# Column sums of a 32768 x 2048 array: adds folded in halves, loads on the GpSimd queue, column blocks on TensorE column groups

## The chip, the cores and the metric

The kernel runs on one core of a Trainium2 chip. The metric is the device time of one execution in microseconds (us).

## The reference

The input `grad_output` has the shape 32 x 1024 x 2048 in fp32 (268.4 MB). The output is the sum over the first two axes, one value for each of 2048 columns:

```
np.sum(grad_output, axis=(0, 1)).astype(np.float32)
```

In what follows the input is a matrix of 32768 rows and D = 2048 columns. A "row" in the text is 128 of these, one in each SBUF partition: 8 KB a partition, 1.05 MB in all. There are 256 such rows.

## The kernel before, in words

**Loads.** 31 bulk loads of 8 rows each (64 KB a partition, contiguous in memory; L69) go out from the SP queue, then a tail of 4, 2 and 1 rows (L87), and a last row in four quarters of 512 columns (L97). A pool gives three buffers of 8 rows (L34); the tail and the last row share one of them. A load into a buffer waits until all that read its earlier content is done.

**Adds.** VectorE keeps one accumulator `acc` of 128 x 2048. For each row of a bulk tile it adds the row to `acc` (L79 for the first, L81 for the others): 8 adds of 2048 columns a tile, and 3 in the last bulk tile.

**TensorE.** What VectorE leaves is summed over the partitions, and added up, by matmuls with a matrix of ones (`mm`, L49 and L50): the last 5 rows of the last bulk tile (`PE_ROWS_LAST`), the 7 tail rows, `acc` and the last row. `sum_row` (L56 to L63) cuts a row into SPLIT = 4 quarters and each quarter into GROUPS = 4 pieces of C = 128 columns. Piece g of each quarter goes to column group g of TensorE, which is PSUM partitions 32 g to 32 g + 31. All four groups so get 384 columns for `head` and 128 for `last` of each row. The ones are 128 x 32, and the 32 output partitions of a group hold the same sums. An fp32 matmul stands in the trace as two, each with its weight load.

**Order.** Each queue runs its instructions in the order of the program, and the framework puts in the waits between engines. On TensorE the order is that of the source: 5 rows of the last bulk tile, 4 tail rows, `acc` (L93), the 2 and the 1 tail rows, then the quarters of the last row as they land.

**End.** ScalarE copies `head` (L105) and VectorE `last` (L106) to `res`, and two stores, from the ScalarE queue (L108) and from SP (L111), write one partition of each group to the output.

Of the kernel before, what the change touches and what calls it, by code (L numbers as in the profile page):

```python
# [1 line left out]

# [4 lines left out]

P = 128
ROWS = 8  # L10
GROUPS = 4
SPLIT = 4
TAIL = (4, 2, 1)
PE_ROWS_LAST = 5


@with_exitstack
def kernel(
    ctx: ExitStack,
    tc: tile.TileContext,  # L20
    grad_output: bass.AP,
    out: bass.AP,
):
    nc = tc.nc
    fp32 = mybir.dt.float32
    D = out.shape[-1]
    flat = grad_output.rearrange("b s d -> (b s) d")
    R = flat.shape[0]
    W = D // SPLIT
    C = W // GROUPS  # L30
    n_bulk = (R // P - sum(TAIL) - 1) // ROWS
    assert (n_bulk * ROWS + sum(TAIL) + 1) * P == R

    io_pool = ctx.enter_context(tc.tile_pool(name="io", bufs=3))  # L34
    const_pool = ctx.enter_context(tc.tile_pool(name="const", bufs=1))
    psum_pool = ctx.enter_context(tc.tile_pool(name="psum", bufs=1, space=bass.MemoryType.PSUM))

    ones = const_pool.tile([P, 32], fp32)
    nc.vector.memset(ones[:], 1.0)  # L39
    acc = const_pool.tile([P, D], fp32)  # L40


    head = psum_pool.tile([P, (SPLIT - 1) * C], fp32)
    last = psum_pool.tile([P, C], fp32)
    res = const_pool.tile([P, SPLIT * C], fp32)

    started = set()

    def mm(dst, g, src, stop):  # L49
        nc.tensor.matmul(  # L50
            dst, lhsT=ones[:], rhs=src, start=(g not in started), stop=stop,
            skip_group_check=True,
        )
        started.add(g)

    def sum_row(src):  # L56
        v = src.rearrange("p (k g i) -> p k g i", k=SPLIT, g=GROUPS)
        for g in range(GROUPS):
            q = slice(32 * g, 32 * g + 32)
            mm(head[q, :].rearrange("p (k i) -> p k i", i=C), ("h", g), v[:, : SPLIT - 1, g, :], False)  # L60
        for g in range(GROUPS):
            q = slice(32 * g, 32 * g + 32)
            mm(last[q, :], ("l", g), v[:, SPLIT - 1, g, :], False)  # L63

    row = 0
    for t in range(n_bulk):
        T = io_pool.tile([P, ROWS * D], fp32, tag="T", name=f"t{t}")
        src = flat[row : row + P * ROWS].rearrange("(p m) d -> p (m d)", p=P)
        nc.sync.dma_start(out=T[:], in_=src)  # L69
        row += P * ROWS  # L70
        on_pe = PE_ROWS_LAST if t == n_bulk - 1 else 0
        for j in range(ROWS):
            part = T[:, j * D : (j + 1) * D]
            if j >= ROWS - on_pe:
                sum_row(part)
            elif t == 0 and j == 0:
                continue
            elif t == 0 and j == 1:
                nc.vector.tensor_add(out=acc[:], in0=T[:, :D], in1=part)  # L79
            else:  # L80
                nc.vector.tensor_add(out=acc[:], in0=acc[:], in1=part)  # L81

    T = io_pool.tile([P, ROWS * D], fp32, tag="T", name="tail")
    at = 0
    for i, m in enumerate(TAIL):
        src = flat[row : row + P * m].rearrange("(p m) d -> p (m d)", p=P)
        nc.sync.dma_start(out=T[:, at * D : (at + m) * D], in_=src)  # L87
        row += P * m
        for j in range(m):
            sum_row(T[:, (at + j) * D : (at + j + 1) * D])  # L90
        at += m
        if i == 0:
            sum_row(acc[:])  # L93

    for k in range(SPLIT):
        dst = T[:, at * D + k * W : at * D + (k + 1) * W]
        nc.sync.dma_start(out=dst, in_=flat[row : row + P, k * W : (k + 1) * W])  # L97
        for g in range(GROUPS):
            q = slice(32 * g, 32 * g + 32)
            into = head[q, k * C : (k + 1) * C] if k < SPLIT - 1 else last[q, :]  # L100
            mm(into, ("h" if k < SPLIT - 1 else "l", g), dst[:, g * C : (g + 1) * C], k >= SPLIT - 2)

    o = out.rearrange("(k g i) -> g k i", k=SPLIT, g=GROUPS)
    n = (SPLIT - 1) * C
    nc.scalar.copy(out=res[:, :n], in_=head[:])  # L105
    nc.vector.tensor_copy(out=res[:, n:], in_=last[:])  # L106
    rows = res[:].rearrange("(g r) c -> g r c", r=32)[:, 0, :]
    nc.scalar.dma_start(  # L108
        out=o[:, : SPLIT - 1, :], in_=rows[:, :n].rearrange("g (k i) -> g k i", i=C)
    )  # L110
    nc.sync.dma_start(out=o[:, SPLIT - 1, :], in_=rows[:, n:])  # L111


# [1 line left out]
_INS = ['grad_output']  # L115
_OUTS = [((2048,), 'float32')]


# [23 lines left out]
```

## Time and profile before

| what | value |
|---|---|
| median of 10 runs | 630.09 us (629.85 to 630.75) |
| the profiled execution's own time | 630.49 us |
| its span, from the first to the last instruction | 628.6 us |
| VectorE busy | 555.0 us (88%), 244 instructions |
| TensorE busy (matmuls) | 16.6 us (3%), 240 instructions |
| data queue (q1), share of the 16 DMA engines' time | 98.9% |
| read from memory | 268.44 MB, 427 GB/s over the span |
| first load's landing | 22.70 us |
| last load's landing | 624.87 us |
| median time from a bulk load's issue to its landing | 39.4 us |

The profile is of one execution. Its span leaves out what lies around the first and the last instruction, so the execution's own time is 1.89 us longer. PE is TensorE's matmuls, PEld its weight loads, DVE is VectorE, ACT ScalarE, POOL GpSimd, SP SyncE; L81 is line 81 of the kernel. A group of instructions reads: line, engine, operation, out<-in, shapes, count, busy time and mean of one in ns, idle time of the engine just before, and what ended most of it.

### The profile page before, as it was taken

What the parts mean: (1) busy time and instruction counts of PE and PEld (TensorE: products, weight loads), DVE (VectorE), ACT (ScalarE), POOL (GpSimd) and SP (SyncE); (2) the same over time, 40 slices, a digit from 0 to 9 for tenths busy, and PEclk for the clock granted to TensorE, in tenths of its full rate; (3) what the DMA queues carried; (4) which work ended last, traced back from release to release, by engine and by line L of the source; (5) the groups of instructions that cost most, each with busy time, mean ns of one, the idle gap of its engine ahead of it and who ended that gap; (6) DMA issues with size and microseconds to landing.
All of it is one profiled execution on the core that took longest, in us unless ns stands there. A gap on an engine that the chain in (4) does not pass through costs nothing.

```text
span 628.6 us, 874 instructions
## 1 busy us (share of the span) xinstructions
PE 16.6 (3%) x240; PEld 8.5 (1%) x240; DVE 555.0 (88%) x244; ACT 1.8 (0%) x2; POOL 0.2 (0%) x4
## 2 busy tenths in 40 slices
PE   0000000000000000000000000000000000000046
PEld 0000000000000000000000000000000000000023
DVE  0579999999899999999999999999999999999980
ACT  0000000000000000000000000000000000000000
POOL 0000000000000000000000000000000000000000
PEclk9999999999999999999999999999999999999998
DMA  9999999999999999999999999999999999999996
GB/s 400 409 459 409 459 417 450 417 450 418 446 421 446 421 446 413 455 413 455 413 455 413 455 413 455 409 459 401 467 400 467 400 467 400 467 400 467 400 432 242
DMA packets 5500, 268.50 MB, mean 427 GB/s; under 512 B 616, under 2 KB 632, under 8 KB 1144
## 3 DMA queue, kind: packets, MB, share of 16 engines
q1 hardware_dynamic: 5480, 268.44, 98.9%
q8 instruction: 2, 0.03, 0.0%
q14 instruction: 2, 0.02, 0.0%
q10 hardware_dynamic: 16, 0.01, 0.0%
HBM read 268.44 MB, written 0.01 MB: 427 GB/s over the span
## 4 chain that ended last, share of the span: by engine, by line
DMA 69%; DVE 29%; issue 0%; SPq 0%; PE 0%; DVEq 0%
DMA t<-in_grad_output_dram 63%; DVE acc L81 29%; DMA tail<-in_grad_output_dram 6%; SPq L97 0%; SPq L87 0%; PE last L50 0%; SPq L69 0%; DVE res L106 0%; DVEq L81 0%
## 5 line engine op out<-in xcount | busy, mean ns | idle before, releaser
L81 DVE TENSOR_TENSOR acc<-acc,t 128x2048 f32<-128x2048 f32 x241 | 552.3, 2292 | 34.9 <-DMA t<-in_grad_output_dram 27.7
L50 PE MATMUL head<-t,ones 128*32 128x384 f32 x40 | 5.9, 661 | 605.3 <-DMA t<-in_grad_output_dram 605.3
L79 DVE TENSOR_TENSOR acc<-t 128x2048 f32<-128x2048 f32 x1 | 2.3, 2291 | 21.8 <-DMA t<-in_grad_output_dram 21.8
L106 DVE COPY res<-last 128x128 f32<-128x128 f32 x1 | 0.3, 293 | 13.2 <-PE last L50 13.2
L50 PEld LDWEIGHTS head<-t,ones 128*32 128x32 f32 x40 | 1.6, 143 | 605.3 <-DVE acc L81 605.3
L50 PE MATMUL head<-tail,ones 128*32 128x384 f32 (+1 forms) x80 | 8.3, 497 | 3.2 <-DMA tail<-in_grad_output_dram 3.1
L50 PE MATMUL last<-tail,ones 128*32 128x128 f32 x64 | 3.8, 311 | 0.2 <-DMA tail<-in_grad_output_dram 0.2
L50 PEld LDWEIGHTS head<-tail,ones 128*32 128x32 f32 x80 | 2.6, 123 | 3.8 <-DMA tail<-in_grad_output_dram 3.8
L50 PE MATMUL last<-t,ones 128*32 128x128 f32 x40 | 2.6, 332 | 0.0
L50 PEld LDWEIGHTS last<-tail,ones 128*32 128x32 f32 x64 | 2.3, 127 | 4.1 <-issue 3.6
L105 ACT COPY res<-head 128x384 f32<-128x384 f32 x1 | 0.5, 478 | 622.8 <-PE head L50 622.8
L50 PEld LDWEIGHTS last<-t,ones 128*32 128x32 f32 x40 | 1.7, 137 | 3.0 <-issue 3.0
L105 ACT ACT_TABLE_LOAD x1 | 1.3, 1283 | 0.7 <-PEq L126 0.7
L50 PE MATMUL head<-acc,ones 128*32 128x384 f32 x8 | 0.8, 486 | 0.0
L39 DVE MEMSET ones<- 128x32 f32 x1 | 0.1, 85 | 0.8 <-PEq L126 0.8
L50 PE MATMUL last<-acc,ones 128*32 128x128 f32 x8 | 0.4, 272 | 0.0
L50 PEld LDWEIGHTS last<-acc,ones 128*32 128x32 f32 x8 | 0.3, 110 | 0.4 <-issue 0.4
L50 PEld LDWEIGHTS head<-acc,ones 128*32 128x32 f32 x8 | 0.2, 110 | 0.0
L126 POOL MEMSET const-bfloat16-1.0<- 128x1 bf16 x1 | 0.1, 102 | 0.0
L126 POOL MEMSET const-uint8-127<- 128x1 uint8 x1 | 0.1, 102 | 0.0
L126 POOL MEMSET const-float32-1.0<- 128x1 f32 x1 | 0.1, 99 | 0.0
L126 POOL MEMSET const-float32-0.0<- 128x1 f32 x1 | 0.1, 98 | 0.2 <-issue 0.2
## 6 DMA issues: line engine op xcount, KB each, us to landing
tail<-in_grad_output_dram SPq DMA_DIRECT2D x1, 4096.0 KB
tail<-in_grad_output_dram SPq DMA_DIRECT2D x1, 2048.0 KB, 34.2
tail<-in_grad_output_dram SPq DMA_DIRECT2D x1, 1024.0 KB, 36.3
tail<-in_grad_output_dram SPq DMA_DIRECT2D x4, 256.0 KB, 36.7
t<-in_grad_output_dram SPq DMA_DIRECT2D x31, 39.4
out_dram<-res ACTq DMA_DIRECT2D x1, 6.0 KB
out_dram<-res SPq DMA_DIRECT2D x1, 2.0 KB
```

What stands on the lines that cost most here:

```text
L39: nc.vector.memset(ones[:], 1.0)
L50: nc.tensor.matmul(dst, lhsT=ones[:], rhs=src, start=(g not in started), stop=stop, skip_group_check=True,)
L79: nc.vector.tensor_add(out=acc[:], in0=T[:, :D], in1=part)
L81: nc.vector.tensor_add(out=acc[:], in0=acc[:], in1=part)
L105: nc.scalar.copy(out=res[:, :n], in_=head[:])
L106: nc.vector.tensor_copy(out=res[:, n:], in_=last[:])
L126: nc = _bacc.Bacc("TRN2", target_bir_lowering=False, num_devices=1)
```

## The change

The work is divided anew.

- *Loads.* 26 tiles of 8 rows, then tiles of 7, 7, 6, 6, 5, 5, 4 and 2 rows (`FOLDED`), a tile of 3 rows (`DIRECT`) and the last 3 rows. The first tile's load stays on SP; all others are issued from the GpSimd queue. The buffers are still three; each of these tiles takes one, and the last 3 rows take one together.
- *Adds.* VectorE folds each tile in place: one wide instruction adds the second half of its rows to the first half, and so on, until one row is left (for 8 rows: 4, 2 and 1 rows wide), and adds this one to `acc`. For odd counts the middle row stays for the next step. The first tile's last fold writes `acc`. In all there are 132 adds; before there were 242.
- *TensorE.* The ones are 128 x 1, so a result has one partition. Of the columns, 0 to 511 go to column group 1, 512 to 1023 to group 2, 1024 to 1535 to group 3 (`LEFT`), 1536 to 1791 to group 0 and 1792 to 2047 to group 1 (`RIGHT`), each block in a PSUM bank of its own. TensorE sums the 3 `DIRECT` rows, then `acc`, then the last 3 rows. The last 3 come as four loads: columns 0 to 1535 of two rows and of one row, then columns 1536 to 2047 of two rows and of one row; their matmuls are in the order left, then right.
- *End.* ScalarE copies blocks 0, 2 and 4 and VectorE blocks 1 and 3 into partition 0 of `acc`, and one store from SP writes the 8 KB. A copy of one element at the start makes ScalarE load its table there.

```
--- before.py
+++ after.py
@@ -7,11 +7,14 @@
 from concourse._compat import with_exitstack
 
 P = 128
-ROWS = 8
-GROUPS = 4
-SPLIT = 4
-TAIL = (4, 2, 1)
-PE_ROWS_LAST = 5
+
+
+
+FOLDED = (8,) * 26 + (7, 7, 6, 6, 5, 5, 4, 2)
+DIRECT = (3,)
+LAST = 3
+LEFT = ((0, 512, 1), (512, 512, 2), (1024, 512, 3))
+RIGHT = ((1536, 256, 0), (1792, 256, 1))
 
 
 @with_exitstack
@@ -26,89 +29,84 @@
     D = out.shape[-1]
     flat = grad_output.rearrange("b s d -> (b s) d")
     R = flat.shape[0]
-    W = D // SPLIT
-    C = W // GROUPS
-    n_bulk = (R // P - sum(TAIL) - 1) // ROWS
-    assert (n_bulk * ROWS + sum(TAIL) + 1) * P == R
+    assert (sum(FOLDED) + sum(DIRECT) + LAST) * P == R
 
     io_pool = ctx.enter_context(tc.tile_pool(name="io", bufs=3))
     const_pool = ctx.enter_context(tc.tile_pool(name="const", bufs=1))
     psum_pool = ctx.enter_context(tc.tile_pool(name="psum", bufs=1, space=bass.MemoryType.PSUM))
 
-    ones = const_pool.tile([P, 32], fp32)
+    ones = const_pool.tile([P, 1], fp32)
     nc.vector.memset(ones[:], 1.0)
+    warm = const_pool.tile([1, 1], fp32)
+    nc.scalar.copy(out=warm[:], in_=ones[0:1, :])
     acc = const_pool.tile([P, D], fp32)
 
 
-    head = psum_pool.tile([P, (SPLIT - 1) * C], fp32)
-    last = psum_pool.tile([P, C], fp32)
-    res = const_pool.tile([P, SPLIT * C], fp32)
 
+    sums = {}
+    for b, (lo, n, g) in enumerate(LEFT + RIGHT):
+        bank = psum_pool.tile([P, 512], fp32, tag=f"ps{b}", name=f"ps{b}")
+        sums[lo] = bank[32 * g : 32 * g + 1, :n]
     started = set()
 
-    def mm(dst, g, src, stop):
-        nc.tensor.matmul(
-            dst, lhsT=ones[:], rhs=src, start=(g not in started), stop=stop,
-            skip_group_check=True,
-        )
-        started.add(g)
-
-    def sum_row(src):
-        v = src.rearrange("p (k g i) -> p k g i", k=SPLIT, g=GROUPS)
-        for g in range(GROUPS):
-            q = slice(32 * g, 32 * g + 32)
-            mm(head[q, :].rearrange("p (k i) -> p k i", i=C), ("h", g), v[:, : SPLIT - 1, g, :], False)
-        for g in range(GROUPS):
-            q = slice(32 * g, 32 * g + 32)
-            mm(last[q, :], ("l", g), v[:, SPLIT - 1, g, :], False)
+    def add(src, pieces, base=0, stop=False):
+        for lo, n, g in pieces:
+            nc.tensor.matmul(
+                sums[lo], lhsT=ones[:], rhs=src[:, lo - base : lo - base + n],
+                start=(lo not in started), stop=stop,
+            )
+            started.add(lo)
 
     row = 0
-    for t in range(n_bulk):
-        T = io_pool.tile([P, ROWS * D], fp32, tag="T", name=f"t{t}")
-        src = flat[row : row + P * ROWS].rearrange("(p m) d -> p (m d)", p=P)
-        nc.sync.dma_start(out=T[:], in_=src)
-        row += P * ROWS
-        on_pe = PE_ROWS_LAST if t == n_bulk - 1 else 0
-        for j in range(ROWS):
-            part = T[:, j * D : (j + 1) * D]
-            if j >= ROWS - on_pe:
-                sum_row(part)
-            elif t == 0 and j == 0:
-                continue
-            elif t == 0 and j == 1:
-                nc.vector.tensor_add(out=acc[:], in0=T[:, :D], in1=part)
-            else:
-                nc.vector.tensor_add(out=acc[:], in0=acc[:], in1=part)
 
-    T = io_pool.tile([P, ROWS * D], fp32, tag="T", name="tail")
-    at = 0
-    for i, m in enumerate(TAIL):
-        src = flat[row : row + P * m].rearrange("(p m) d -> p (m d)", p=P)
-        nc.sync.dma_start(out=T[:, at * D : (at + m) * D], in_=src)
-        row += P * m
+    def load(m, lo=0, hi=D, at=None, advance=True, queue=None):
+        nonlocal row
+        n = hi - lo
+        if at is None:
+            at = io_pool.tile([P, 8 * D], fp32, tag="T", name=f"t{row}_{lo}")[:, : m * n]
+        src = flat[row : row + P * m].rearrange("(p m) d -> p m d", p=P)[:, :, lo:hi]
+        (queue or nc.gpsimd).dma_start(out=at.rearrange("p (m d) -> p m d", m=m), in_=src)
+        if advance:
+            row += P * m
+        return at
+
+    for i, m in enumerate(FOLDED):
+        T = load(m, queue=nc.sync if i == 0 else None)
+        while m > 1:
+            h = m // 2
+            into = acc[:] if i == 0 and m == 2 else T[:, : h * D]
+            nc.vector.tensor_add(out=into, in0=T[:, : h * D], in1=T[:, (m - h) * D : m * D])
+            m -= h
+        if i:
+            nc.vector.tensor_add(out=acc[:], in0=acc[:], in1=T[:, :D])
+
+    for m in DIRECT:
+        T = load(m)
         for j in range(m):
-            sum_row(T[:, (at + j) * D : (at + j + 1) * D])
-        at += m
-        if i == 0:
-            sum_row(acc[:])
+            add(T[:, j * D : (j + 1) * D], LEFT + RIGHT)
+    add(acc[:], LEFT + RIGHT)
 
-    for k in range(SPLIT):
-        dst = T[:, at * D + k * W : at * D + (k + 1) * W]
-        nc.sync.dma_start(out=dst, in_=flat[row : row + P, k * W : (k + 1) * W])
-        for g in range(GROUPS):
-            q = slice(32 * g, 32 * g + 32)
-            into = head[q, k * C : (k + 1) * C] if k < SPLIT - 1 else last[q, :]
-            mm(into, ("h" if k < SPLIT - 1 else "l", g), dst[:, g * C : (g + 1) * C], k >= SPLIT - 2)
-
-    o = out.rearrange("(k g i) -> g k i", k=SPLIT, g=GROUPS)
-    n = (SPLIT - 1) * C
-    nc.scalar.copy(out=res[:, :n], in_=head[:])
-    nc.vector.tensor_copy(out=res[:, n:], in_=last[:])
-    rows = res[:].rearrange("(g r) c -> g r c", r=32)[:, 0, :]
-    nc.scalar.dma_start(
-        out=o[:, : SPLIT - 1, :], in_=rows[:, :n].rearrange("g (k i) -> g k i", i=C)
-    )
-    nc.sync.dma_start(out=o[:, SPLIT - 1, :], in_=rows[:, n:])
+    T = io_pool.tile([P, 8 * D], fp32, tag="T", name="last")
+    cut, at, left, right = RIGHT[0][0], 0, [], []
+    first = row
+    for lo, hi, into in ((0, cut, left), (cut, D, right)):
+        row = first
+        for m in (LAST - 1, 1):
+            n = hi - lo
+            S = load(m, lo, hi, T[:, at : at + m * n])
+            into += [S[:, j * n : (j + 1) * n] for j in range(m)]
+            at += m * n
+    for j, S in enumerate(left):
+        add(S, LEFT, stop=j == LAST - 1)
+    for j, S in enumerate(right):
+        add(S, RIGHT, base=cut, stop=j == LAST - 1)
+    res = acc[0:1, :]
+    for k, (lo, n, g) in enumerate(LEFT + RIGHT):
+        if k in (0, 2, 4):
+            nc.scalar.copy(out=res[:, lo : lo + n], in_=sums[lo])
+        else:
+            nc.vector.tensor_copy(out=res[:, lo : lo + n], in_=sums[lo])
+    nc.sync.dma_start(out=out[None, :], in_=res)
 
 
 # ---- launch: one core; inputs and outputs as the reference has them ----
```

## The prediction

> **What bounds the kernel now.** I read, in this order: the page's parts 2 to 4, the loads' windows, the waits of the queue and of VectorE, then the timeline of the last 25 us. The page first.
>
> ```profile
> DMA  9999999999999999999999999999999999999996
> DMA packets 5500, 268.50 MB, mean 427 GB/s; under 512 B 616, under 2 KB 632, under 8 KB 1144
> q1 hardware_dynamic: 5480, 268.44, 98.9%
> q8 instruction: 2, 0.03, 0.0%
> q14 instruction: 2, 0.02, 0.0%
> DMA 69%; DVE 29%; issue 0%; SPq 0%; PE 0%; DVEq 0%
> L81 DVE TENSOR_TENSOR acc<-acc,t 128x2048 f32<-128x2048 f32 x241 | 552.3, 2292 | 34.9 <-DMA t<-in_grad_output_dram 27.7
> ```
>
> The 16 DMA engines are busy in every slice but the last. The chain names VectorE for 29%, but only because each new load waits for a buffer; VectorE itself waits for data. The windows (columns: stretch and length; PE, PEld, DVE, ACT, POOL busy; clock; DMA share; GB/s) give the rate of three loads each:
>
> ```profile
> 217.20:275.26 58.06, 0.00 (x0) 0.00 (x0) 55.00 (x24) 0.00 (x0) 0.00 (x0) 1.00 1.00 433
> 391.35:450.38 59.03, 0.00 (x0) 0.00 (x0) 55.00 (x24) 0.00 (x0) 0.00 (x0) 1.00 1.02 443
> ```
>
> 58.05 / 3 = 19.35 us for 8 rows of 1.05 MB, 2.419 us a row. The longer window is one engine's: its landing marks in the trace fall behind the other 15 by 0.98 us at 143 us and again at 434 us, where an 8 KB packet of q14 (VectorE's instructions) stands between its data packets. A load has landed when its last engine has.
>
> ```profile
> SPq L69 <- DVE acc L81: 520.0, 28, 19.0
> DVE acc L81 <- DMA t<-in_grad_output_dram: 27.7, 30, 3.2
> ```
>
> The queue waits up to 19.0 us for VectorE, yet load to landing has a median of 39.4 us: when a buffer comes free, two loads are still under way. So folding faster can't start data sooner. The kernel is bound by its bytes, and only its end is free to move:
>
> ```profile
> 607.02 1.53 PE L50 MATMUL head<-t,ones 128*32 128x384 f32 x8
> 608.73 1.16 PE L50 MATMUL head<-t,ones 128*32 128x384 f32 x8
> 610.78 0.83 PE L50 MATMUL head<-t,ones 128*32 128x384 f32 x8
> 624.91 0.42 PE L50 MATMUL last<-tail,ones 128*32 128x128 f32 x8 [0.20 <-DMA tail<-in_grad_output_dram]
> 625.40 0.29 DVE L106 COPY res<-last 128x128 f32<-128x128 f32 x1 [13.15 <-PE last L50]
> 625.73 0.65 SPq L111 DMA_DIRECT2D out_dram<-res  x1
> ```
>
> One row on TensorE (four column groups at once, 512 columns each) took 608.73 - 607.02 = 1.71 us early, and 0.86 us later (the row ahead of the third line began at 609.92). TensorE kept up: the last data landed at 624.87 and its work was over 0.47 us later. From the last copy's end (625.70) to the span's end (628.6) there are 2.90 us.
>
> **What the Trainium skill says.** "DMA: Bandwidth & Descriptors", section "Issuing engines are not separate DMA queues": loads from any queue run on the same 16 engines. So the move to GpSimd buys no bandwidth by itself. No run here shows a load from that queue; the same page's "Specifications" give it about 1 us to the first byte against 0.6 us. In the trace SP's first load was issued at 0.73 and its first packet started at 1.74 us, 1.0 us.
> "SBUF — State Buffer", section "Who interferes with whom": a two-input add in SBUF doesn't lock GpSimd out of writing descriptors (the page calls this inferred). No run here shows it.
> "TensorE: Matmul & The Clock Gate", Part 1: TensorE runs at half rate until a free-running window of 3.4 us has been busy. The trace agrees: 1.71 us a row until about 609.4, 4.05 us after the first matmul at 605.35, then 0.86.
>
> **The change part by part.**
> *Folding.* 132 adds in place of 242. An add of 2048 columns starts every 2.325 us, of which 2048/0.96 GHz ("VectorE: DVE Perf Modes", Specifications) is 2.133 and 0.192 the fixed part. An 8-row tile is then 8 x 2.133 + 4 x 0.192 = 17.83 us against 18.60. In the bulk this hides under the 19.35 us of the next load: worth nothing.
> *Queue.* 38 loads go from SP to GpSimd; SP keeps the first, so both start together and nothing else of weight stands in either queue. Issue cost is hidden by the two loads under way, as long as it is below 2 x 19.35 - 17.8 = 20.9 us. I leave the packet time at 2.420 us for 64 KB. The new access pattern names the rows one by one; I take it that a partition's rows still go as one packet.
> *Instruction fetches.* 132 adds and their waits are some 165 instructions, so I expect one q14 fetch, not two: 0.98 us saved on the late engine.
> *Shrinking loads.* A tile of m rows costs m x 2.133 + (adds) x 0.192: 15.70 (7), 13.57 (6), 11.43 (5), 9.11 (4), 4.65 (2). Loads stay as in the trace, 2.419 us a row; I start from the late engine's first landing, 22.70, plus one fetch. The second 7-row tile lands at 541.3, and from there VectorE is never idle: it ends at 557.0, 570.6, 584.2, 595.6, 607.1 and, with the 4-row tile, 616.2; acc is ready at 620.8. The three direct rows land at 616.3. **A new wait**: the last load needs the buffer of the 4-row tile, free at 616.2. Reaction of the software queue: unknown; at least SP's 1.0 us, I take 2.0, at most 5. Gap before the last load: 616.2 + 2.0 - 616.3 = 1.9 us. Its 3 rows need 7.26 us and 0.43 more for 48 short packets an engine (a 2 KB packet took 84 ns, an 8 KB one 313, where 37.6 ns a KB would give 75 and 301: 9 ns each). Last byte at 625.8, against 624.87.
> *TensorE.* The column groups are no longer even. A full row gives group 1 two blocks, 512 + 256 columns; groups 2 and 3 get 512, group 0 256. At 0.86/512 = 1.684 ns a column, group 1 sets the pace: (3 direct rows + acc) x 768 + 3 left x 512 + 3 right x 256 = 5376 columns, 9.05 us. It can't start before 616.3 (L93's earlier rows, which in the kernel before gave TensorE work from 605.35 on, are gone), and starts at half rate. That lasts 3.4 us at best (the page), 4.05 in this trace, 6.8 at worst (start just after a window's edge); I take the middle, 5.1, and lose 5.1 x (1 - 0.86/1.71) = 2.5 us. End of TensorE: 616.3 + 0.1 + 9.05 + 2.5 = **627.95**. It is later than the last byte plus a right row (625.8 + 0.43), so the gap of 1.9 us is hidden behind TensorE; if TensorE had less to do, the gap would be next.
> *End.* 0.06 to notice, a copy of 256 columns 0.29 + 128/0.96 GHz = 0.43, then 2.90 as before; the result leaves as one row of 8 KB (a packet of 313 ns, or 16 of 512 B at 25): 0.15. The warm-up copy hides ScalarE's table load at the start, as now. The span ends at 627.95 + 0.06 + 0.43 + 2.90 + 0.15 = 631.5.
> *Sum.* 631.5 - 628.6 = 2.9 us. Profiled execution: 630.49 + 2.9 = 633.4. The median of the runs is 0.40 below that execution: **633.0 us**.
>
> **The rivals.**
> *Shorter packets (17%).* If rows leave as packets of 8 KB, each takes 313 ns instead of 2420/8 = 302.5: 3.5% of 619 us is 21 us, 654 us; at 4 KB the fixed 9 ns counts twice. For it: the access pattern is split by row, and software writes the descriptors. Against: a full row range is contiguous on both sides. If only part of this happens, from 642 us up.
> *GpSimd held up by the wide adds (9%).* If an add does keep GpSimd from its descriptors, the direct load, wanted at 607.1, waits for the 4-row tile's first add (2 x 2.133 + 0.16 = 4.4 us) or its whole 9.1 us. Nothing is left under way to hide it, and TensorE starts that much later: 637.4 to 642. For it: nothing in this trace; against it, the page above.
> *Not slower (17%).* The software queue might hand each engine its next packet without a pause. The page gives the fabric 435.2 GB/s, so 64 KB would take 2.409 us (an estimate from "DMA: Bandwidth & Descriptors", Specifications) rather than 2.420. Up to the direct rows that is 31.6 x 0.075 = 2.4 us: 630.6, no change; with no fetch on the late engine and the shortest cold stretch, 628.8. It decides at about 2.413 us a packet, where 1.6 us are won. Against it: SP's 98.9% leaves little to win.
>
> **How the numbers follow.** Differences of 0.2% (1.26 us) can be told from no change: below 628.8, 628.8 to 631.4, above. My forecast has 57%: 633.0, own range 631.2 to 635 (cold stretch 3.4 to 6.8 us: -0.8 to +0.8; reaction up to 5 us: the last byte then comes at 628.8 and TensorE ends 629.3, +1.3). All of it but 2% is slower. The two slow rivals add 26%; the third splits into 12% same and 5% faster. Slower 0.55 + 0.26 = 0.81, same 0.14, faster 0.05. For 8 in 10 the range takes in the forecast, the held-up GpSimd and most of the no-change case, and leaves out the shorter packets and the faster tail: 629.5 to 642.
>
> **What would show it.** Right: packets of 64 KB at 2.42 us on the new queue; VectorE without idle time from about 541 us; direct rows landing near 616 and TensorE working without a break from then to 2 us after the last byte; a gap of DMA near 616. Wrong: a mean of bytes over time below 420 GB/s in the bulk (short packets); late starts of loads behind wide adds; TensorE waiting for data at the end.

## The result, and the profile after

The changed kernel takes 643.84 us (median of 8 runs, 643.46 to 644.32) against 630.13 us for the kernel before (29 runs): a ratio of 1.0217, 95% interval 1.0208 to 1.0226. It is 2.2% slower, 13.7 us, where 633.0 us was predicted. The span grew from 628.6 to 642.0 us, 13.4 us.

From the page of the changed kernel: the span, DMA's busy tenths in 40 slices and its rate, the packets, the queues (packets, MB, share of the 16 engines' span), and the chain's shares.

```profile
span 642.0 us, 404 instructions
DMA  9997799999999999999999999999999999999995
DMA packets 5684, 268.46 MB, mean 418 GB/s; under 512 B 625, under 2 KB 625, under 8 KB 1201
q0 software_dynamic: 5536, 260.05, 94.1%
q1 hardware_dynamic: 146, 8.40, 3.1%
q14 instruction: 2, 0.02, 0.0%
DMA 60%; DVE 34%; issue 5%; PE 0%; POOL 0%; POOLq 0%
```

The kernel before showed 9s up to the last slice. Here the fourth and fifth slices, 48 to 80 us, are at 7: the DMA engines stood idle early, once. The number of packets hardly changed, and the trace's 64 KB packets on q0 last 2.420 us, as on SP's queue. The loss isn't in the rate of the transfers. The mean of 418 GB/s lies below the 420 that the prediction named as the sign of short packets, but idle time brings it down, not short packets. The windows of the changed kernel show where it is (columns as in the prediction's windows):

```profile
40.00:60.00 20.00, 0.00 (x0) 0.00 (x0) 20.00 (x3) 0.00 (x0) 0.00 (x0) 1.00 0.97 419
61.50:69.40 7.90, 0.00 (x0) 0.00 (x0) 7.90 (x3) 0.00 (x0) 0.53 (x1) 1.00 0.00 0
80.00:100.00 20.00, 0.00 (x0) 0.00 (x0) 19.43 (x6) 0.00 (x0) 1.06 (x2) 1.00 1.03 446
```

For 7.9 us nothing moves, while VectorE is busy throughout. In the trace's landing marks, loads 0 and 1 land at 39.71 and 42.12, load 2 at 61.47 and load 3 at 90.33 us: 28.86 instead of 19.35 us after the one ahead. The timeline of the changed kernel's start (start, duration, engine, line, operation, count, idle time before and its releaser) says why:

```profile
0.74 0.40 SPq L68 DMA_DIRECT2D t<-in_grad_output_dram  x1
1.25 1.20 POOL L68 DMA_DIRECT2D t<-in_grad_output_dram  x2 [0.80 <-POOLq L124]
39.73 25.96 DVE L78 TENSOR_TENSOR t<-t 128x8192 f32<-128x8192 f32 x4 [38.86 <-DMA t<-in_grad_output_dram]
65.61 2.28 DVE L78 TENSOR_TENSOR acc<-t 128x2048 f32<-128x2048 f32 x1
67.82 10.88 DVE L78 TENSOR_TENSOR t<-t 128x2048 f32<-128x2048 f32 x2
68.19 0.53 POOL L68 DMA_DIRECT2D t<-in_grad_output_dram  x1 [65.75 <-DVE acc L78]
```

Tile 0 has three folds, two within `t` and one into `acc`. But *four* stand ahead of the one into `acc`: two of them are tile 1's. VectorE's program after the build isn't in the order of the source. Its beginning (program lines, no profile; t_0_74 is tile 0, t_0_79 tile 1, t_0_85 tile 2):

```
L78 t_0_74<-t_0_74 128x8192
L78 t_0_79<-t_0_79 128x8192
L78 t_0_74<-t_0_74 128x4096
L78 t_0_79<-t_0_79 128x4096
L78 acc<-t_0_74 128x2048
L78 t_0_79<-t_0_79 128x2048
L78 t_0_85<-t_0_85 128x8192
L81 acc<-acc,t_0_79 128x2048
```

From there on each tile is finished before the next, up to the last two folded tiles. Load 3 needs tile 0's buffer. It comes free at 65.61 + 2.28 = 67.89, 6.42 us after load 2 has landed and left nothing under way. GpSimd issues load 3 at 68.19, its first packet starts at 69.42, and the load lands 20.91 us after it, where loads that follow one another land 19.35 us apart: 6.42 + 1.53 + 1.56 = 9.51 us. (The first load of the kernel before, which also started with nothing under way, took 20.96 us from its first packet to its landing.)

The timeline of the changed kernel's end:

```profile
613.58 2.29 DVE L81 TENSOR_TENSOR acc<-acc,t 128x2048 f32<-128x2048 f32 x1
615.79 8.94 DVE L78 TENSOR_TENSOR t<-t 128x4096 f32<-128x4096 f32 x3
624.65 4.61 DVE L81 TENSOR_TENSOR acc<-acc,t 128x2048 f32<-128x2048 f32 x2
626.62 5.11 PE L54 MATMUL ps<-t,ones 128*1 128x512 f32 x29 [626.62 <-DMA t<-in_grad_output_dram]
627.23 2.52 POOL L68 DMA_DIRECT2D last<-in_grad_output_dram  x4 [10.54 <-DVE acc L81]
634.38 3.07 PE L54 MATMUL ps<-last,ones 128*1 128x512 f32 x18 [1.15 <-DMA last<-in_grad_output_dram]
637.72 1.46 PE L54 MATMUL ps<-last,ones 128*1 128x256 f32 x12 [0.27 <-DMA last<-in_grad_output_dram]
639.22 0.41 DVE L108 COPY acc<-ps 1x256 f32<-1x256 f32 x1 [1.01 <-PE ps L54]
639.72 0.32 SPq L109 DMA_DIRECT2D out_dram<-acc  x1
```

The same once more: the 2-row tile's fold (the third of the x3) stands ahead of the add that frees the 4-row tile's buffer, 2.3 us. The last loads are issued at 627.23, after the direct rows have landed at 626.48; the last byte lands at 638.30 against 624.87, and TensorE waits for it (1.15 and 0.27 us).

So the 13.4 us of span are: 8.3 at the landing of the 26th tile (516.73 against 508.42: 9.5 of gap, less the 1.2 or so by which the slowest DMA engine lags less), 5.1 from there to the last byte (121.57 against 116.44), and nothing after it.

### The profile page after: what moved, and what is told of

It reads as the page before. It is cut to its first block, busy times and chain, and to the rows that moved or that the text cites. A ratio compares the mean times of both kernels' runs of the same rounds, so it can differ in the third digit from the quotient of the medians.

```text
span 642.0 us, 404 instructions
## 1 busy us (share of the span) xinstructions
PE 11.0 (2%) x70; PEld 2.4 (0%) x70; DVE 551.9 (86%) x135; ACT 3.0 (0%) x5; POOL 20.8 (3%) x42
## 4 chain that ended last, share of the span: by engine, by line
DMA 60%; DVE 34%; issue 5%; PE 0%; POOL 0%; POOLq 0%
DMA t<-in_grad_output_dram 59%; DVE t L78 29%; DVE acc L81 5%; DMA last<-in_grad_output_dram 1%; PE ps L54 0%; POOL last L68 0%; DVE acc L108 0%; POOLq L68 0%
## 5 line engine op out<-in xcount | busy, mean ns | idle before, releaser
L78 DVE TENSOR_TENSOR t<-t 128x2048 f32<-128x2048 f32 (+3 forms) x98 | 473.7, 4838 | 76.6 <-DMA t<-in_grad_output_dram 74.6
L81 DVE TENSOR_TENSOR acc<-acc,t 128x2048 f32<-128x2048 f32 x33 | 75.6, 2291 | 1.1
L68 POOL DMA_DIRECT2D t<-in_grad_output_dram x34 | 18.1, 533 | 598.1 <-DVE acc L81 531.6
L54 PE MATMUL ps<-t,ones 128*1 128x512 f32 (+1 forms) x30 | 5.3, 680 | 626.6 <-DMA t<-in_grad_output_dram 626.6
L106 ACT COPY acc<-ps 1x512 f32<-1x512 f32 (+1 forms) x3 | 1.5, 506 | 635.9 <-PE ps L54 635.9
L54 PE MATMUL ps<-last,ones 128*1 128x512 f32 (+1 forms) x30 | 4.4, 506 | 1.6 <-DMA last<-in_grad_output_dram 1.4
L68 POOL DMA_DIRECT2D last<-in_grad_output_dram x4 | 2.5, 637 | 10.5 <-DVE acc L81 10.5
L54 PE MATMUL ps<-acc,ones 128*1 128x512 f32 (+1 forms) x10 | 1.9, 506 | 0.0
## 6 DMA issues: line engine op xcount, KB each, us to landing
t<-in_grad_output_dram POOLq DMA_DIRECT2D x1, 2048.0 KB, 13.7
```

Of the source, the lines that this page charges most:

```text
L54: nc.tensor.matmul(sums[lo], lhsT=ones[:], rhs=src[:, lo - base : lo - base + n], start=(lo not in started), stop=stop,)
L68: (queue or nc.gpsimd).dma_start(out=at.rearrange("p (m d) -> p m d", m=m), in_=src)
L78: nc.vector.tensor_add(out=into, in0=T[:, : h * D], in1=T[:, (m - h) * D : m * D])
L81: nc.vector.tensor_add(out=acc[:], in0=acc[:], in1=T[:, :D])
L106: nc.scalar.copy(out=res[:, lo : lo + n], in_=sums[lo])
```

## The experiments

**Theory A**: the time goes to the order of VectorE's adds where two tiles land together, with the loads of two queues started at once. **Rivals**: the software queue is slower, the wide adds hold GpSimd up, or folding itself is late. All ratios are against the kernel before, on the same chips (630.2 us); "last byte" is the last landing in the profiled execution.

| kernel | time, us | ratio (95% interval) | last byte, us |
|---|---|---|---|
| changed | 643.84 | 1.0217 (1.0208 to 1.0226) | 638.30 |
| e1: changed, adds in source order | 633.16 | 1.0053 (1.0038 to 1.0068) | 627.04 |
| e2: changed, all loads on GpSimd | 635.29 | 1.0079 (1.0063 to 1.0096) | 629.88 |
| e3: changed, all loads on SP | 633.92 | 1.0059 (1.0044 to 1.0074) | 628.67 |
| e4: changed, last loads wait for no fold | 642.64 | 1.0195 (1.0180 to 1.0210) | 634.29 |
| e5: before, folded | 630.02 | 0.9996 (0.9987 to 1.0004) | 624.91 |
| e6: before, SP then GpSimd | 629.77 | 0.9993 (0.9984 to 1.0001) | 624.36 |
| e7: e8 with the first tiles alternating | 635.29 | 1.0083 (1.0068 to 1.0099) | 629.43 |
| e8: all on SP, source order | 632.80 | 1.0040 (1.0027 to 1.0054) | 626.11 |
| e9: e8, last loads wait for no fold | 632.96 | 1.0038 (1.0025 to 1.0051) | 625.00 |
| e10: e9, even column groups | 631.88 | 1.0025 (1.0015 to 1.0034) | 625.09 |
| e11: before, all bulk tiles folded | 629.48 | 0.9988 (0.9981 to 0.9995) | 623.77 |
| e12: e11, SP then GpSimd | 629.50 | 0.9986 (0.9980 to 0.9993) | 623.51 |

**e1: the source's order.**

```
-            nc.vector.tensor_add(out=into, in0=T[:, : h * D], in1=T[:, (m - h) * D : m * D])
+            tc.keep_in_program_order(
+                nc.vector.tensor_add(out=into, in0=T[:, : h * D], in1=T[:, (m - h) * D : m * D])
+            )
...
-            nc.vector.tensor_add(out=acc[:], in0=acc[:], in1=T[:, :D])
+            tc.keep_in_program_order(nc.vector.tensor_add(out=acc[:], in0=acc[:], in1=T[:, :D]))
```

> The changed kernel, with VectorE's adds kept in the order of the source (no alternating between two tiles). Theory A: the loss at the start comes from the alternating order on top of two loads sharing the DMA engines. Tile 0 still lands near 39.7, but is folded by 55.3, so the fourth load starts before the third ends at 61.2: no gap, 9.5 us less; at the end the 4-row tile comes free 2.3 us sooner: 632.0. Theory B, the loss lies in the GpSimd queue itself (descriptors held up, slow restart) or in the sharing alone: 641 to 644.

The same lines of the timeline, for e1:

```profile
1.24 1.20 POOL L68 DMA_DIRECT2D t<-in_grad_output_dram  x2 [0.80 <-POOLq L126]
39.59 13.15 DVE L79 TENSOR_TENSOR t<-t 128x8192 f32<-128x8192 f32 x2 [38.72 <-DMA t<-in_grad_output_dram]
52.77 2.29 DVE L79 TENSOR_TENSOR acc<-t 128x2048 f32<-128x2048 f32 x1
55.36 0.53 POOL L68 DMA_DIRECT2D t<-in_grad_output_dram  x1 [52.92 <-DVE acc L79]
```

Load 3 is issued at 55.36 instead of 68.19, 6 us before load 2 lands, and the loads land at 39.56, 41.97, 61.33 and 80.69: no gap. The time falls by 10.7 us. Both queues, the wide adds and the shrinking tiles are as in the changed kernel, so none of these alone makes the loss.

**e2 and e3: one queue.** e2 issues the first load from GpSimd too, e3 puts all loads on SP.

```
-        T = load(m, queue=nc.sync if i == 0 else None)
+        T = load(m)
```
```
-        (queue or nc.gpsimd).dma_start(out=at.rearrange("p (m d) -> p m d", m=m), in_=src)
+        nc.sync.dma_start(out=at.rearrange("p (m d) -> p m d", m=m), in_=src)
```

> The changed kernel with the first load on the GpSimd queue too, so that one queue holds all loads in order. Theory A: tile 0 lands at about 23 to 24 us, no sharing, no gap near 61 us; the gap at the end stays: 634.3. Theory B (the GpSimd queue is slow): no better than 643, and worse if the first load starts late.

> The changed kernel with all loads on the SP queue. Theory A: the queue as such costs nothing but a slower reaction of 0.7 us at the end: no gap near 61 us, 633.5. Theory B (the GpSimd queue is at fault for both gaps): 630 to 631.

With one queue the loads land one by one from 23.51 us (e2) and 22.6 us (e3), and the first tiles' adds stand in source order, without being told to. The timeline of e2:

```profile
23.53 13.15 DVE L78 TENSOR_TENSOR t<-t 128x8192 f32<-128x8192 f32 x2 [22.66 <-DMA t<-in_grad_output_dram]
36.72 2.29 DVE L78 TENSOR_TENSOR acc<-t 128x2048 f32<-128x2048 f32 x1
39.30 0.53 POOL L68 DMA_DIRECT2D t<-in_grad_output_dram  x1 [36.34 <-DVE acc L78]
```

Either queue alone gives back 8.6 to 9.9 us. The 1.4 us between e2 and e3 are about the 0.9 us by which GpSimd's first load is later, and 0.3 us more at the last loads. The alternation of the last two tiles is still there in both: e3 is 1.1 us slower than e8, which is e3 in source order (their intervals overlap).

**e4: the last loads wait for no fold.** The last three rows go to the upper part of the direct rows' buffer, which is free.

```
+    T = io_pool.tile([P, 8 * D], fp32, tag="T", name="end")
     for m in DIRECT:
-        T = load(m)
+        load(m, at=T[:, : m * D])
...
-    T = io_pool.tile([P, 8 * D], fp32, tag="T", name="last")
-    cut, at, left, right = RIGHT[0][0], 0, [], []
+    cut, at, left, right = RIGHT[0][0], sum(DIRECT) * D, [], []
```

> The changed kernel with the last 3 rows loaded into the free part of the direct tile's buffer, so that their load waits for nothing more than the direct load does. The gap at the start stays. Theory A with TensorE next in line: the last byte comes 4.1 us sooner, at about 634.2, but TensorE, which starts at 626.6 and has 9.05 us of work at full rate plus some 1.6 for a slow start, ends at 637.3 instead of 639.2: 641.9. Rival, TensorE is no bound: 639.7.

The last byte comes 4.0 us sooner, 634.29, and the time falls by 1.2 us only: the matmuls now run from 626.27 to 637.5 without waiting for data. So TensorE is next, as expected, though the gain is 0.7 us smaller than the expected one (641.9).

**e5 and e6: parts of the change in the kernel before.** e5 folds the first 30 bulk tiles, e6 moves all loads but the first to GpSimd.

```
+        if t < n_bulk - 1:
+            m = ROWS
+            while m > 1:
+                m //= 2
+                into = acc[:] if t == 0 and m == 1 else T[:, : m * D]
+                nc.vector.tensor_add(out=into, in0=T[:, : m * D], in1=T[:, m * D : 2 * m * D])
+            if t:
+                nc.vector.tensor_add(out=acc[:], in0=acc[:], in1=T[:, :D])
+            continue
```
```
-        nc.sync.dma_start(out=T[:], in_=src)
+        (nc.gpsimd if t else nc.sync).dma_start(out=T[:], in_=src)
...
-        nc.sync.dma_start(out=T[:, at * D : (at + m) * D], in_=src)
+        nc.gpsimd.dma_start(out=T[:, at * D : (at + m) * D], in_=src)
...
-        nc.sync.dma_start(out=dst, in_=flat[row : row + P, k * W : (k + 1) * W])
+        nc.gpsimd.dma_start(out=dst, in_=flat[row : row + P, k * W : (k + 1) * W])
```

> The kernel before with the folding alone: the first 30 bulk tiles are folded in halves (4 wide adds a tile), all else as before, on the SP queue. Both theories: the bulk hides it. Only the number of VectorE's instructions changes what the DMA engines do: one fetch of 8 KB in place of two on the late engine, 0.98 us less: 629.1. If folding delayed any load: above 630.5.

> The kernel before with the queue alone: first load on SP, all other loads on the GpSimd queue. The adds all go through acc, so their order can't alternate. The first two loads share the DMA engines and land near 40 and 42 us; tile 0 is added by 40 + 18.6 = 58.3, the fourth load starts at about 59.9, before the third ends at 61.2. Theory A (sharing does harm only together with the alternating order): 630.1 to 630.6. Theory that sharing alone makes the gap: 638 to 640.

Folding alone: no difference. The expectation of 629.1 is a miss by 0.9 us: the page of e5 has one q14 packet, as expected, but the last byte landed as before.

```profile
q8 instruction: 2, 0.03, 0.0%
q14 instruction: 1, 0.01, 0.0%
```

In the profiled execution the saving was there and was used up. At the 26th tile the slowest DMA engine landed 1.1 us behind the first, against 2.6 in the kernel before. Two things took it back. In this execution, the slowest of e5's 13, the 64 KB packets between 22 and 80 us took 2.45 us rather than 2.42, and load 3 landed 0.7 us later than in the kernel before; why isn't known. And after the first of the two q8 packets (16 KB, 1.1 and 0.9 us, at 617.8 and 624.0 us) the slowest engine was 1.9 us behind. I take q8 for TensorE's instructions: the kernels with 240 matmuls in the trace have two such packets, those with 160 one, those with 70 none.

Two queues alone: no difference either, though the first two loads land at 39.56 and 41.97 as in the changed kernel. In e6 every add goes into `acc`, so their order can't change. Timeline of e6:

```profile
41.91 53.46 DVE L81 TENSOR_TENSOR acc<-acc,t 128x2048 f32<-128x2048 f32 x23
56.12 0.53 POOL L69 DMA_DIRECT2D t<-in_grad_output_dram  x1 [53.68 <-DVE acc L81]
```

**e7 and e8: the order alone.** All loads on SP; e8 has all adds in source order (e3's and e1's edits), e7 has the first three tiles' adds in the changed kernel's order and all others in source order (`steps` yields a tile's adds one by one).

```
...
+    first = [steps(i, FOLDED[i], load(FOLDED[i])) for i in range(3)]
+    for i in (0, 1, 0, 1, 0, 1, 2, 1, 2, 2, 2):
+        into, x, y = next(first[i])
+        tc.keep_in_program_order(nc.vector.tensor_add(out=into, in0=x, in1=y))
...
```

> All loads on SP, with VectorE's adds of the first three tiles in the alternating order of the changed kernel, all others in source order. Tile 0 lands at 22.7, but its second add stands behind tile 1's first, which waits for the landing at 42.0: tile 0 comes free at 61.8 instead of 38. The fourth load starts 2.0 us late and restarts 0.7 slower: 2.7 us above the same kernel in source order, so about 634.7 with that at 632.0. Theory that the alternating order alone makes the whole gap: 9.5 above it.

> The changed kernel with all loads on SP and VectorE in source order: neither sharing nor alternating, at the start or the end. 2 us below all on SP with the alternating end (633.9): 632.0. What is left above the kernel before (630.2) is then the shrinking loads and TensorE's end.

The timeline of e8's start, with tile 0 done before load 1 lands:

```profile
22.63 13.15 DVE L79 TENSOR_TENSOR t<-t 128x8192 f32<-128x8192 f32 x2 [21.77 <-DMA t<-in_grad_output_dram]
35.82 2.29 DVE L79 TENSOR_TENSOR acc<-t 128x2048 f32<-128x2048 f32 x1
```

The timeline of e7: VectorE waits 10.66 us for tile 1 before it may go on with tile 0.

```profile
22.61 8.69 DVE L85 TENSOR_TENSOR t<-t 128x8192 f32<-128x8192 f32 x1 [21.76 <-DMA t<-in_grad_output_dram]
41.97 17.36 DVE L85 TENSOR_TENSOR t<-t 128x8192 f32<-128x8192 f32 x3 [10.66 <-DMA t<-in_grad_output_dram]
59.25 2.28 DVE L85 TENSOR_TENSOR acc<-t 128x2048 f32<-128x2048 f32 x1
```

Tile 0 is free at 61.53, 0.2 us after load 2's landing at 61.31; load 3 lands at 83.42, against 80.67 in e8, and the time is 2.5 us more. So the order alone costs 2.5, the common start alone nothing (e6), and both together some 9.5. They draw on the same slack. In source order tile 0 is free at 38.1 with one queue, against 61.3 for the landing of load 2 (23 us to spare), and at 55.06 with two (6.3 us to spare); the two folds of tile 1 that are put ahead take 13.

The end of e8 is the end that the prediction described. Its timeline:

```profile
612.76 2.29 DVE L83 TENSOR_TENSOR acc<-acc,t 128x2048 f32<-128x2048 f32 x1
615.08 2.62 SPq L68 DMA_DIRECT2D last<-in_grad_output_dram  x4
617.42 5.83 PE L54 MATMUL ps<-t,ones 128*1 128x512 f32 x29 [617.42 <-DMA t<-in_grad_output_dram]
624.60 4.03 PE L54 MATMUL ps<-last,ones 128*1 128x512 f32 x28
628.28 0.41 DVE L110 COPY acc<-ps 1x256 f32<-1x256 f32 x1 [0.18 <-PE ps L54]
629.05 0.32 SPq L111 DMA_DIRECT2D out_dram<-acc  x1
```

TensorE works from the direct rows' landing to 628.63 without a wait for data, 2.5 us past the last byte (626.11).

**e9 and e10: what sets that end.** e9 is e8 with e4's edit; e10 moves one block of columns to another column group as well.

```
-RIGHT = ((1536, 256, 0), (1792, 256, 1))
+RIGHT = ((1536, 256, 0), (1792, 256, 0))
```

> The kernel of e8 (all loads from SP, adds in source order) with the last three rows loaded into the upper part of the direct tile's buffer, so that the last load waits for no fold. Theory A (TensorE's column group with 768 columns a row is the bound at the end of e8, so the earlier last byte stays hidden behind it): last byte near 624.9, the matmuls run without a break from about 617.4 to about 628, time 632.0 to 632.8 against 632.8 for e8. Rival (the last load's wait sets the end): TensorE follows the last byte by 0.5 us and the time falls to about 630.5.

> The kernel of e9 with the fifth column block moved from column group 1 to group 0, so that a full row gives each of the four groups 512 columns. Theory A (uneven groups are the bound at the end): (3 direct rows + acc) x 512 + 3 x 512 = 3584 columns in each group instead of 5376 in one, 3.0 us less of matmuls at full rate; then the last byte sets the end, and the time is 1 to 1.5 us below e9, near 631. Rival (the cold start, or anything else than the share of columns, sets the pace): as e9 within 0.4 us.

e9: last byte 1.1 us sooner, time the same. The wait for the 4-row tile's buffer is hidden behind TensorE, as the prediction had it. e10 is 1.1 us below e9, within the 1 to 1.5 expected (their intervals overlap a little; the spans differ by 1.5), and in its trace TensorE waits for data, which it never does in e9's: the uneven groups were the bound. 1.7 us to the kernel before remain. The timeline of e10:

```profile
616.70 5.13 PE L54 MATMUL ps<-end,ones 128*1 128x512 f32 x30 [616.70 <-DMA end<-in_grad_output_dram]
624.50 2.24 PEld L54 LDWEIGHTS ps<-end,ones 128*1 128x1 f32 x12 [0.17 <-DMA end<-in_grad_output_dram]
626.86 0.41 DVE L110 COPY acc<-ps 1x256 f32<-1x256 f32 x1 [0.84 <-PE ps L54]
627.29 0.36 ACT L108 COPY acc<-ps 1x256 f32<-1x256 f32 x1 [0.81 <-PE ps L54]
```

Group 0 waits for the right columns, whose first two rows land at 624.46. But then all that is left, 3 rows of 512 columns, belongs to group 0 alone: 3 x 0.86 = 2.6 us, to 627.1. In the kernel before, a last quarter row of 128 columns in each of four groups was left, 0.47 us after the last byte.

**e11 and e12: a version that takes the folding alone.** e11 folds all 31 bulk tiles, gives TensorE no row of the last one and sums `acc` after the tail rows; e12 has e6's queues as well.

```
-        on_pe = PE_ROWS_LAST if t == n_bulk - 1 else 0
-        for j in range(ROWS):
...
+        m = ROWS
+        while m > 1:
+            m //= 2
+            into = acc[:] if t == 0 and m == 1 else T[:, : m * D]
+            tc.keep_in_program_order(
+                nc.vector.tensor_add(out=into, in0=T[:, : m * D], in1=T[:, m * D : 2 * m * D])
+            )
+        if t:
+            tc.keep_in_program_order(nc.vector.tensor_add(out=acc[:], in0=acc[:], in1=T[:, :D]))
...
-        if i == 0:
+        if i == len(TAIL) - 1:
```

> The kernel before with all 31 bulk tiles folded on VectorE in source order, no row of the last bulk tile on TensorE, and acc summed after the 4-, 2- and 1-row loads. Theory A (folding is worth a fetch of instructions at most): 629.2 if with 320 rather than 480 matmul instructions TensorE's late fetches miss the last load, else 630.2. Rival (VectorE's fold of the last bulk tile, ready about 18 us after it lands, comes too late): acc is ready near 617.5, seven us before the last byte, so no loss; above 631 if it is.

> The kernel of e11 with the first load from SP and all others from GpSimd. Theory A (the mixed start costs nothing once the adds stand in source order): as e11 within 0.4 us, loads 0 and 1 landing near 40 and 42, then 61.3 and 80.7 without a gap. Rival (the mixed start costs by itself): 8 to 10 us more, near 638.

Both are 0.12 to 0.14% faster than the kernel before, some 0.7 us. The intervals exclude no change, but the gain is less than the 0.2% that the prediction took as the bound of what can be told. The gain has the size of a fetch of instructions, which is read from the traces and not tested by itself. The queues of e11:

```profile
q8 instruction: 1, 0.02, 0.0%
q14 instruction: 2, 0.01, 0.0%
```

One q8 packet, not two; the second of the q14 comes at 628 us, after the work. The slowest engine is 1.6 us behind the first at the 26th tile, where the kernel before has 2.6 and TensorE has not begun. Up to there the folding and the fetch that it saves are all that e11 changes. The only q8 packet, at 622.1 us, takes none of it back: at the last landing the lag is 1.5, and the last byte lands at 623.77, 1.1 us sooner. e12 lands its first two loads at 39.56 and 41.96 and the next at 61.3 and 80.67: with the order kept, the common start is free, as in e6.

## Why the prediction was wrong, step by step

*Queue: the step that failed.* The prediction let "both start together" and put the move at nothing, with the issue cost "hidden by the two loads under way". Both did start together, and issue cost was hidden. But a common start has two consequences that the step left out, and the prediction took the adds to stand in the order of the source without saying so. The 16 engines take packets of both queues in turn, so load 0 lands at 39.7 instead of 22.7 us, with load 1 right behind. That takes 17 us out of the slack between the release of tile 0 and the landing of load 2 (still 6.3 us to spare in e1, 5.5 in e6). And the folds, which unlike adds into `acc` don't depend on each other across tiles, are put in alternating order when two tiles come from different queues; that takes 13 us where 6.3 were left. The price of the step is some 9.5 us, against nothing in the prediction. "Hidden by the two loads under way" was read from the steady state; at the start the first two loads land together, and then only one is under way.

Only the framework's order is shown, not its reason: one queue gave the source's order at the start (e2), two queues gave the alternating one. At the end, where all loads come from one queue, the last two tiles alternate all the same, in e3 too, and nothing in the runs says why.

*Shorter packets; not slower.* Neither rival came: packets stayed at 2.420 us for 64 KB, as the forecast took them, and e1 and e8 differ by 0.4 us with overlapping intervals. The Trainium skill's "DMA: Bandwidth & Descriptors", section "Issuing engines are not separate DMA queues", is borne out: e12 with two queues takes 629.50 us, e11 with one 629.48. That they also delay the first of two loads follows from it, and I didn't draw it.

*GpSimd held up by the wide adds.* Not seen: GpSimd issues load 3 0.3 us after its release in the changed kernel and in e1, with an add under way on VectorE, and just as late in e2, where VectorE stands idle (39.01 to 39.30). The Trainium skill's inferred remark in "SBUF — State Buffer", section "Who interferes with whom", holds in these traces.

*Folding.* Held: e5 shows no difference. Its price held too: in e1 a tile of 8 rows took 17.71 us from the start of its first add to the start of the next tile's (54.98 to 72.69), against 17.83 in the prediction.

*Instruction fetches.* Half held. In e5, e8 and e9 one q14 packet came during the work, as predicted; in the changed kernel two did, at 249 and 584 us. The second goes with the queue: every kernel here that issues its loads from GpSimd has one between 562 and 590 us, and none with all loads on SP has. That it fetches GpSimd's instructions is a guess. At the 26th tile, before it, the slowest engine lagged by 1.3 us, against 2.6 in the kernel before.

*Shrinking loads.* Close where the order is the source's: in e8 the direct rows landed at 617.29 (616.3 predicted), the 4-row tile's buffer was free at 615.05 (616.2), the last byte came at 626.11 (625.8). GpSimd's reaction, from the end of the add to the first packet, was 1.7 us in e1 and in the changed kernel; 2.0 was taken. What was missed is the alternation of the last two tiles: 2.1 us at the last byte (119.51 us from the 26th tile in e1, 121.57 in the changed kernel), and in the time 1.2 us, since e4, which takes the whole wait away, wins no more before TensorE is next.

*TensorE.* Held: 9.05 us of columns in group 1 and 2.5 of cold start were 11.6 us; e8 shows 628.63 - 617.42 = 11.2. The half-rate stretch wasn't one figure: by the granted clock in the traces it lasted 2.6 us from the first matmul in the changed kernel, 4.1 in e8 and 5.7 in e9. The Trainium skill's "TensorE: Matmul & The Clock Gate", Part 1, speaks of a free-running window of 3.4 us; the spread agrees with its free-running, but the 2.6 us is shorter than one window.

*End.* 2.90 + 0.15 us from the last copy to the end of the span became 2.35 (639.63 to 641.98): the one store of one row is 0.5 us better than the two, not 0.15 worse. Over all runs the kernels with one store took 2.25 to 2.35 us here, those with two 2.6 to 3.2.

*Sum.* In e1, the changed kernel with its adds in source order, the span is 631.1 and the time 633.16; the prediction had 631.5 and 633.0. So the forecast was that of the kernel in source order. That the span fits to 0.4 us is in part luck: against the forecast the direct rows landed 0.9 us late, TensorE took 0.45 us less and the end 0.9 us less. Of the 10.7 us on top, 9.2 stand at the landing of the 26th tile (516.73 against 507.53); the rest is the end. Of the 2.5 and 2.7 us that e8 and e9 lose to the kernel before, 1.1 are the uneven groups (e10); of the 1.7 that remain in e10, what is due to TensorE's late, cold start and what to the right rows in one group wasn't told apart.

## What to carry to other kernels

Before saying that a new queue or fewer adds are "hidden by the loads under way", work out the first round by itself: when each buffer first comes free, against the landing of the last load that didn't need one. When in-place steps on several buffers no longer depend on each other, read the order in which they stand on the engine, and pin it: an order that cost 2.5 us here where loads landed one by one (e7) cost 9.5 where they landed together. And count what is left on the last engine after the last byte by the group that has most of it.

## What the runs showed of the hardware

The first packets after an idle stretch last longer: 2.5 to 3.3 us for 64 KB at 69.4 us in the changed kernel, against 2.420; for the 6 KB packets of the last loads up to 1.5 us against 0.23, while in e4, where these loads waited behind others, none took over 0.4. From an add's end to the first packet of the load that waits for it, GpSimd took 1.5 (load 3) to 1.7 us (last loads), SP 1.46 (last loads of e8). A fetch of instructions stands between the data packets of one DMA engine and holds up each load that this engine takes part in: in the kernel before, two packets of 8 KB put it 0.98 us behind each, and after one 16 KB packet of 1.1 us in e5 the slowest engine's lag grew from 1.1 to 1.9 us.
